# A hybrid encoder block: five convolution pairs by Strassen instead of three, and thirty Lo blocks made during attention

## The chip, the core and the metric

The kernel runs on one core of one Trainium2 chip. A core has TensorE (PE in the profile; its weight loads are PEld), VectorE (DVE), ScalarE (ACT), GpSimd (POOL) and SyncE (SP), each with its own instruction queue, worked off in order, and 16 DMA engines that all queues share. The metric is the device time of one execution in microseconds (us), taken as the median of several runs.

## The reference

One layer over 512 tokens of 2048 numbers, in float32:

```python
u = rms_norm(h, mix_pre_g)
q, k, v, ca, cb, ga, gb = split(u @ w_in)          # 1024, 1024, 1024, 1024, 1024, 2048, 2048 columns
y_attn = neighbourhood_attention(q, k, v, rpb) @ w_attn_o      # 8 heads of 128
z = depthwise_conv31(ca * sigmoid(cb)) + b_dw
y_conv = silu(layer_norm(z)) @ w_conv_o
merged = sigmoid(ga) * y_attn + sigmoid(gb) * y_conv
h = h + rms_norm(merged @ w_out, mix_post_g)
gate, up = split(rms_norm(h, ffn_pre_g) @ w_gate_up)            # 2 x 5632 columns
h = h + rms_norm((silu(gate) * up) @ w_down, ffn_post_g)
```

## The kernel before

Activations lie transposed: 128 features on the partitions, the 512 tokens along the free dimension. A block is 128 output features; its weights are [128, 2048], two halves of 1024 columns (eight 128 x 128 tiles each).

**Hi and Lo.** Every float32 operand is split: Hi is the value rounded by a ScalarE cast to the type fp32r, Lo is what is left, one VectorE subtraction. A plain product needs three matmuls per weight tile: Hi by Lo, Hi by Hi, Lo by Hi (`gemm`, L198 to L202). `wchunk` (L143) loads 1024 columns of weights into one of five `raw` buffers, casts (`whi`, L152) and subtracts (`wlo`, L157), with three buffers for each. After each chunk it calls `taps(rate)`.

**Strassen pairs.** `strassen` (L271) takes two blocks at once. The 2 x 2 halves of the weights (a11, a12 of the first block, a21, a22 of the second) and of the activations are combined in Winograd's form, so that seven products take the place of eight. `merged` puts Hi and Lo of 256 tokens side by side in one tile, so that a product is eight matmuls of 512 columns with Hi of the weights and eight of 256 with Lo. The products of a normal pair in order: 11 (a11), T2 (s2 = s1 - a11), T1 (s1 = a21 + a22, summed by a DMA), T3 (s3 = a11 - a21), 21 (a12), 22 (s4 = a12 - s2), T4 (a22). `halved_weights` (L255) makes Hi and Lo of each of the seven. Between them VectorE adds in PSUM: y += p1 (L329) after T2, z += u2 (L336) after T1, p5 = y + p5 (L342) after T3, and ScalarE copies (L288). With `turn`, T3 and 22 use Lo ahead of Hi. In the first pair of a product (`apart=True`) product 21 comes second, into a bank of its own, and v += p1 (L338) joins it later; there 22 follows T3 directly. Five places have such a first pair: the gates (g), w_out (wo), the FFN's gate and up (f5), and the two parts of w_down (d, twice).

**Stages.** (1) The first four projections of the convolution, while x arrives. (2) Convolution blocks 2 to PLAIN - 1 = 4 as plain pairs cb, ca (loop L534). `conv` (L434) gates a block, `begin_block` (L451) starts its depthwise convolution and queues 30 taps (`todo`); a tap is one VectorE instruction (L473). (3) V in two halves of eight chunks, with `normalize` (L524) making the normalized tiles, four pairs of them (UN_EARLY) ahead of the last plain pair. (4) Eight heads (loop L637): q and k as plain products, then `attention`. The taps of the five blocks run here and before, at `rate` per chunk. (5) Two plain gate blocks, then 17 Strassen pairs (loop L734): convolution blocks 5 to 7, then 14 gate pairs. The convolution inputs of pairs 1 and 2 go to DRAM (`z_d`) and come back when `todo` is short; three or four taps per pair stand behind products that TAP_AT names. (6) 16 attention projections (rate R_Y, then `mean` for the taps that are left, layer norm), 16 convolution projections with the gates and the operands of w_out (`operand_steps`, L849). (7) w_out, (8) the FFN.

**Order.** The program's order is a list schedule: an instruction goes when it is the first in the text that is ready by the scheduler's own model of time. `keep_in_program_order` and `issued_behind` (a plain order of issue, no semaphore) bind it by hand: taps are kept in order, a tap in a pair stands behind a matmul, the loads of the gates behind earlier ones.

Of the kernel before, what the change touches and what calls it, by code (L numbers as in the profile page):

```python
# [25 lines left out]
F32 = mybir.dt.float32  # L26
F32R = mybir.dt.float32r
# [4 lines left out]
P = 128  # L32
# [25 lines left out]
DN_3 = DN_2 + DN_P  # L58

LN_AT = 10  # L60
R_CONV, R_V, R_QK, R_Y = 4, (2, 4), 4, 4
PLAIN = 5
TAP_K, TAP_AT = 2, ((1, 3, 5), (0, 1, 3, 5))
BEFORE = 14
WARM = 17
C0_PARTS = (0, 256), (256, 512), (512, 1024)
# [4 lines left out]
SINGLE, SUMMED = 4, 10  # L71
COPY_AT = 10
RE_EARLY = 11
UN_EARLY, YA_EARLY = 4, 8
SUMMED_AT = 10
C_PRE, C_POST, C_FPRE, C_FPOST, C_LNG, C_LNB, C_BDW, C_WDW = 0, 16, 32, 48, 64, 72, 80, 88
C_N = C_WDW + CT * CW
# [3 lines left out]
def hybrid_block(ctx: ExitStack, tc, xT, vecs, rpb, mask, w_c0, w_qk, w_v, w_gg, w_cg, w_ao, w_co, w_out, w_g0, w_gu, w_dn, w_dl, g_post, out):  # L81
# [32 lines left out]
    def abank(name):  # L114
        return at.tile([P, NT], F32, tag="at", name=name)
# [19 lines left out]
            tc.keep_in_program_order(ins)  # L135

    todo, rate = [], 0

    def wraw(name):
        return wp.tile([P, 1024], F32, tag="raw", name=f"raw_{name}", bufs=5)  # L140

    def wchunk(src, name, parts=((0, 1024),), cast=nc.scalar.copy, raw=None, load=nc.sync.dma_start):
        w = src.shape[-1]  # L143
        loaded = raw is not None
        raw = raw if loaded else wraw(name)[:, :w]
        hi = wp.tile([P, 1024], F32R, tag="whi", name=f"whi_{name}")[:, :w]
        lo = wp.tile([P, 1024], F32R, tag="wlo", name=f"wlo_{name}")[:, :w]
        for s in parts:
            s = slice(*s)
            if not loaded:  # L150
                load(raw[:, s], src[:, s])
            ins = cast(hi[:, s], raw[:, s])  # L152
            if len(parts) > 1:
                tc.keep_in_program_order(ins)
        for s in parts:
            s = slice(*s)
            nc.vector.tensor_tensor(out=lo[:, s], in0=raw[:, s], in1=hi[:, s].bitcast(F32), op=ALU.subtract)  # L157
        taps(rate)
        return hi, lo

    def split(src, name, scale=None, pin=False):
# [21 lines left out]
    def gemm(outs, acts, name, n=None, more=None, cols=slice(0, NT), between=(), pin=False, raw=None, load=nc.sync.dma_start, at=None):  # L183

        n = n or len(acts)
        between = iter(between)
        for c in range(0, n, 8):
            w = min(8, n - c)
            while len(acts) < c + w:
                acts.append(more(len(acts)))  # L190
            for i, (ps, src) in enumerate(outs):
                hi, lo = wchunk(src[:, c * P : (c + w) * P], f"{name}_{i}_{c}", raw=None if c or i else raw, load=load)
                for k in range(w):
                    (at or {}).get((c, i, k), lambda: None)()
# [3 lines left out]
                    mmul = nc.tensor.matmul(ps, hi[:, s], al, start=first, stop=False)  # L198
                    if pin and k == 0:
                        tc.keep_in_program_order(mmul)  # L200
                    nc.tensor.matmul(ps, hi[:, s], ah, start=False, stop=False)  # L201
                    nc.tensor.matmul(ps, lo[:, s], ah, start=False, stop=last)  # L202
                next(between, lambda: None)()

    def interleaved(ps, hi, lo, acts, c, cols=slice(0, NT)):
# [46 lines left out]
        load(raw, w[:, c * 1024 : (c + 1) * 1024])  # L252
        return raw

    def halved_weights(w, name, pin=False, after=None):  # L255

        hi = wp.tile([P, 1024], F32R, tag="whi", name=f"{name}h")
        lo = wp.tile([P, 1024], F32R, tag="wlo", name=f"{name}l")
        ins = nc.scalar.copy(hi, w), nc.vector.tensor_tensor(out=lo, in0=w, in1=hi.bitcast(F32), op=ALU.subtract)  # L259
        for i in ins if pin else ():  # L260
            tc.keep_in_program_order(i)
        if after:
            issued_behind(ins[1], after)
        return hi, lo
# [3 lines left out]
        a11 = quarter(w0, 0, name)  # L268
        return (a11, *halved_weights(a11, name))

    def strassen(w0, w1, op, name, n, s1=None, behind_last=None, first=None, quarters=None, apart=False, turn=True, midway=None, taps_at=(), after=None):  # L271

# [5 lines left out]

        def wsum(a, b, op, i):
            t = stp.tile([P, 1024], F32, tag="S", name=f"{name}s{i}")
            nc.vector.tensor_tensor(out=t, in0=a, in1=b, op=op)
            return t

        def copied(ps, i):
# [49 lines left out]
        nc.vector.tensor_tensor(out=z, in0=z, in1=u2, op=ALU.add)  # L336
# [5 lines left out]
        nc.vector.tensor_tensor(out=p5, in0=y, in1=p5, op=ALU.add)  # L342
        s4 = s2
        nc.vector.tensor_tensor(out=s4, in0=a12, in1=s2, op=ALU.subtract)
# [187 lines left out]

    rate = R_CONV
    for i in range(2, PLAIN):  # L534
        if i == PLAIN - 1:
            for c in range(UN_EARLY):
                normalize(c)
        pb, pa = abank(f"cb{i}"), abank(f"ca{i}")
        gemm([(pb, w_cg[CT + i])], u, f"cb{i}", between=() if i > 2 else (first_convs,))
        gemm([(pa, w_cg[i])], u, f"ca{i}")  # L540
        conv(i, pa, pb)

# [90 lines left out]
        nc.scalar.copy(o, po)  # L633
        nc.gpsimd.dma_start(att_d[h], o)  # L634
# [97 lines left out]

    op = operands(b11, b2, t12, t34)
    for n in range(CT - PLAIN + KT - 2):  # L734
        gate = n >= CT - PLAIN
        i = n - (CT - PLAIN) + 2 if gate else n + PLAIN
        w0, w1 = (2 * CT + i, 2 * CT + KT + i) if gate else (CT + i, i)
        if n:
            s1, quarters = sums(w_cg[w1], f"g{n}", load_in_order) if n == 1 else None, None
        c11, c12, c21, c22 = strassen(  # L740
            w_cg[w0], w_cg[w1], op, f"g{n}", n + 1, s1, quarters=quarters, first=None if n else first, apart=n == 0,
            midway=None if n else plain_gates, taps_at=TAP_AT[n % 2] if n else (),
        )
        if i == KT - 1:

# [775 lines left out]
```

## Time and profile before

| | before |
|---|---|
| three runs, us | 2476.03, 2477.77, 2477.32 (median 2477.32) |
| profiled execution, us | 2478.54 |
| its span, us | 2476.7 |
| mean granted TensorE clock | 0.998 |
| DMA moved, MB | 476.00 |

The span runs from the first to the last instruction of one profiled execution. A line of the profile's groups reads: line, engine, operation, tiles written and read, count, then busy time, the mean of one in ns, and idle time of the engine just before them with what ended it. A line of the waits reads: who, for whom, us in total, times, longest. A line of the order of time reads: start, duration (with matmuls that are alike put together), engine, line, tiles. A stretch's line gives, per engine, busy time and number of instructions, then the clock, the busy share of the DMA engines and GB/s. Where the stages lie, by the starts of TensorE's instructions: first plain pair 51.0, last plain pair 95.6, V 118.6, QK and attention 207.1, plain gates from about 415, first g pair 461.9, y 794.7, first wo pair 972.3, f5 1251, the two d parts 2059 and 2259.

### The profile page before, as it was taken

To read this page: it belongs to the slowest core of one execution; us is meant where nothing else is said; L and a number is where in the kernel's file an instruction comes from. 1 tells how busy PE (TensorE), PEld (TensorE's weight loads), DVE (VectorE), ACT (ScalarE), POOL (GpSimd) and SP (SyncE) were. 2 spreads that over 40 slices of the span, in tenths; PEclk is the share of its full clock that TensorE was granted. 3 is DMA by queue.
4 is the path that set the end of the run, shared out by engine and by line. 5 is a ranking of instruction groups with operands and counts; after the bars stand their busy time and mean duration, and the time that the engine had idled before them with its cause. 6 is when DMAs were issued, how large, how long until landed. Compare 5 with 4: busy or idle time off the path is not lost. (4 is left out here: it accounts for less than half of the span.)

```text
span 2476.7 us, 35648 instructions
## 1 busy us (share of the span) xinstructions
PE 2454.9 (99%) x13219; PEld 2123.7 (86%) x13219; DVE 2080.8 (84%) x2756; ACT 1262.5 (51%) x1951; POOL 481.9 (19%) x574
## 2 busy tenths in 40 slices
PE   9999999999999999999999999999999999999998
PEld 7888888888888887889888888888888888888887
DVE  5998754998989778878998888889988889989886
ACT  5233333655555344556555555555555565556554
POOL 0102312200000000012111111222221203532343
PEclk9999999999999999999999999999999999999999
DMA  6363224866667543769466655667666678888987
GB/s 216 125 205 104 103 90 133 253 189 195 187 196 232 187 140 123 205 211 307 147 178 179 184 174 168 184 199 203 209 210 190 215 226 247 239 224 256 213 222 221
DMA packets 162958, 476.00 MB, mean 192 GB/s; under 512 B 18528, under 2 KB 28224, under 8 KB 162784
## 3 DMA queue, kind: packets, MB, share of 16 engines
q1 hardware_dynamic: 107200, 334.41, 40.4%
q0 software_dynamic: 33840, 101.34, 19.2%
q10 hardware_dynamic: 21744, 37.98, 4.1%
q8 instruction: 104, 1.70, 0.3%
q14 instruction: 70, 0.57, 0.1%
HBM read 400.52 MB, written 72.22 MB: 191 GB/s over the span
## 5 line engine op out<-in xcount | busy, mean ns | idle before, releaser
L473 DVE SCALAR_TENSOR_TENSOR cv<-z,vec,cv 128x497 f32<-128x497 f32 (+9 forms) x180 | 137.7, 766 | 2.8
L1058 POOL TENSOR_TENSOR row<-row,asq 128x512 f32<-128x512 f32 x30 | 55.0, 1832 | 406.6 <-ACT asq L1057 406.6
L157 DVE TENSOR_TENSOR wlo_qk<-raw_qk,whi_qk 128x1024 fp32r<-128x1024 f32 x32 | 39.9, 1247 | 57.3 <-ACT whi_qk L152 57.3
L1219 POOL TENSOR_TENSOR ys<-ys,row 128x512 f32<-128x512 f32 x32 | 57.7, 1802 | 119.6 <-DVE ys L355 109.2
L152 ACT CAST whi_qk<-raw_qk 128x1024 fp32r<-128x1024 f32 x32 | 33.6, 1051 | 81.2 <-PE qk L201 44.4
L1082 POOL TENSOR_TENSOR an<-an,row 128x512 f32<-128x512 f32 x32 | 54.0, 1688 | 72.8 <-DMA an<-a_d 46.4
L152 ACT CAST whi_y<-raw_y 128x1024 fp32r<-128x1024 f32 x31 | 32.6, 1052 | 66.4 <-PE py L201 50.9
L572 POOL TENSOR_TENSOR bm<-braw,msk 128x64 f32<-128x64 f32 x96 | 47.1, 526 | 17.3 <-DMA braw<-in_rpb 17.3
L198 PE MATMUL py<-ycl,whi_y 128*128 128x512 f32 x128 | 49.8, 389 | 0.0
L201 PE MATMUL py<-ych,whi_y 128*128 128x512 f32 x128 | 49.8, 389 | 0.0
L202 PE MATMUL py<-ych,wlo_y 128*128 128x512 f32 x128 | 49.8, 389 | 0.0
L157 DVE TENSOR_TENSOR wlo_y<-raw_y,whi_y 128x1024 fp32r<-128x1024 f32 x31 | 37.8, 1221 | 10.6 <-ACT whi_y L152 10.3
L473 DVE SCALAR_TENSOR_TENSOR cv<-zr,vec,cv 128x497 f32<-128x497 f32 (+14 forms) x60 | 45.2, 755 | 0.5
L483 POOL TENSOR_TENSOR csum<-csum,cv 128x512 f32<-128x512 f32 x7 | 12.6, 1803 | 158.9 <-DVE cv L473 149.1
L823 DVE TENSOR_TENSOR gg<-py,gg 128x512 f32<-128x512 f32 x32 | 21.7, 684 | 18.4 <-PE py L202 10.6
L609 ACT ACTIVATE sc<-sc,st 128x256 f32<-128x256 f32 x32 | 16.1, 505 | 31.0 <-DVE st L608 30.2
L1220 POOL DMA_DIRECT2D y_d<-ys x32 | 29.0, 907 | 10.1 <-POOL ys L1219 7.8
L1149 DVE TENSOR_TENSOR sg<-sg,su 128x512 f32<-128x512 f32 x39 | 30.0, 768 | 0.0
L634 POOL DMA_DIRECT2D att_d<-ao x8 | 4.4, 554 | 127.2 <-ACT ao L633 107.0
L201 PEld LDWEIGHTS py<-ych,whi_y 128*128 128x128 f32 x128 | 24.0, 188 | 5.0
L202 PEld LDWEIGHTS py<-ych,wlo_y 128*128 128x128 f32 x128 | 24.0, 188 | 5.0
L198 PEld LDWEIGHTS py<-ycl,whi_y 128*128 128x128 f32 x128 | 24.0, 188 | 4.9
(3251 smaller groups left out, 8656.5 us busy)
## 6 DMA issues: line engine op xcount, KB each, us to landing
raw_qk<-in_w_qk SPq DMA_DIRECT2D x32, 512.0 KB, 3.4
a_d<-sg ACTq DMA_DIRECT2D x41, 256.0 KB, 4.0
raw_v<-in_w_v SPq DMA_DIRECT2D x16, 512.0 KB, 5.2
gg<-g_d SPq DMA_DIRECT2D x32, 256.0 KB, 4.9
raw_y<-in_w_co SPq DMA_DIRECT2D x16, 512.0 KB, 3.6
raw_f<-in_w_g SPq DMA_DIRECT2D x16, 512.0 KB, 4.2
an<-a_d POOLq DMA_DIRECT2D x32, 256.0 KB, 5.5
as_d<-an POOLq DMA_DIRECT2D x32, 256.0 KB, 4.8
```

Of the source, the lines that this page charges most:

```text
L152: ins = cast(hi[:, s], raw[:, s])
L157: nc.vector.tensor_tensor(out=lo[:, s], in0=raw[:, s], in1=hi[:, s].bitcast(F32), op=ALU.subtract)
L198: mmul = nc.tensor.matmul(ps, hi[:, s], al, start=first, stop=False)
L201: nc.tensor.matmul(ps, hi[:, s], ah, start=False, stop=False)
L202: nc.tensor.matmul(ps, lo[:, s], ah, start=False, stop=last)
L473: ins = nc.vector.scalar_tensor_tensor(out=a[:, to], in0=z[:, fr], scalar=col(C_WDW, i * CW + w), in1=a[:, to], op0=ALU.mult, op1=ALU.add)
L572: nc.gpsimd.tensor_tensor(out=bm[:, o + i - i0], in0=raw[:, :, min(max(i, 0), 3) * EC : (min(max(i, 0), 3) + 1) * EC], in1=msk[:, o + i - ...
L1058: nc.gpsimd.tensor_tensor(out=row[n], in0=row[n], in1=sq, op=ALU.add)
L1082: ins = nc.gpsimd.dma_start(t, a_d[DN_P + k]), nc.gpsimd.tensor_tensor(out=t, in0=t, in1=row[k // KT], op=ALU.mult)
L1149: nc.vector.tensor_tensor(out=t, in0=t, in1=up, op=ALU.mult)
L1219: tc.keep_in_program_order(nc.gpsimd.tensor_tensor(out=t, in0=t, in1=row[n], op=ALU.mult))
L1220: tc.keep_in_program_order(nc.gpsimd.dma_start(y_d[0, o], t, accum_op=ALU.add))
```

## The change

- PLAIN goes from 5 to 3: convolution blocks 3 and 4 leave the plain loop and become Strassen pairs, of which there are now 19 (5 convolution, 14 gate).
- With three plain blocks, 90 instead of 150 taps belong to the stages up to attention. R_V goes from (2, 4) to (1, 4). When no taps are left there, `wchunk` calls `lo_ahead` instead: it takes up the blocks loaded at the call before (a ScalarE copy to fp32r, a VectorE subtraction, a store by GpSimd to `lo_d`) and loads the next one or two of them (alternating), each behind the last matmul of the chunk before. 30 blocks: a12 and a22 of pairs 1 to 18, without the first three and the last three.
- In the pairs, those blocks' Lo is loaded from `lo_d` by SP instead of being subtracted by VectorE.
- The 150 taps of the five convolution pairs: TAP_AT names six or seven products per pair (four in pairs 1 and 18); 112 taps run there, 32 in the y stage, 6 in `mean`.
- UN_EARLY goes from 4 to 2, and the early tiles are normalized between cb and ca of the last plain pair.
- VectorE's order in the five first pairs: the Lo of s3 and v += p1 behind y += p1; s4 behind z += u2; the following pair's s2 and s3 behind z += u2.
- Four of the operand steps of w_out for the last tile but one are put ahead of the last gate.

```diff
-R_CONV, R_V, R_QK, R_Y = 4, (2, 4), 4, 4
-PLAIN = 5
-TAP_K, TAP_AT = 2, ((1, 3, 5), (0, 1, 3, 5))
+R_CONV, R_V, R_QK, R_Y = 4, (1, 4), 4, 4
+AHEAD_PER_CHUNK = 1, 2
+PLAIN = 3
+TAP_K, TAP_AT = 2, ((0, 1, 2, 3, 4, 5), (0, 1, 2, 3, 4, 5, 6), (0, 2, 3, 5))
...
-UN_EARLY, YA_EARLY = 4, 8
+UN_EARLY, YA_EARLY = 2, 8
...
+    lo_d = dr.tile([CT - PLAIN + KT - 2, 2, P, 1024], F32, name="lo_d")
+    ahead_of_pairs, loaded, latest, with_pairs = [], [], [None], False
+
+    def lo_ahead():
+
+        for dst, t in loaded:
+            h = sm.tile([P, 1024], F32R, tag="jh", name="jh", bufs=1)
+            for ins in (
+                nc.scalar.copy(h, t),
+                nc.vector.tensor_tensor(out=t.bitcast(F32R), in0=t, in1=h.bitcast(F32), op=ALU.subtract),
+            ):
+                issued_behind(ins, latest[0])
+            nc.gpsimd.dma_start(dst, t)
+        count = AHEAD_PER_CHUNK[len(ahead_of_pairs) % 3 == 0]
+        loaded[:] = []
+        for dst, src in ahead_of_pairs[:count]:
+            t = sm.tile([P, 1024], F32, tag="jr", name="jr", bufs=3)
+            issued_behind(nc.sync.dma_start(t, src), latest[0])
+            loaded.append((dst, t))
+        del ahead_of_pairs[:count]
...
-        taps(rate)
+        if todo or ahead or waiting:
+            taps(rate)
+        elif with_pairs:
+            lo_ahead()
...
-    def halved_weights(w, name, pin=False, after=None):
+    def halved_weights(w, name, pin=False, after=None, lo_src=None):
...
+        if lo_src is not None:
+            nc.scalar.copy(hi, w)
+            nc.sync.dma_start(lo.bitcast(F32), lo_src)
+            return hi, lo
...
         def wsum(a, b, op, i):
             t = stp.tile([P, 1024], F32, tag="S", name=f"{name}s{i}")
-            nc.vector.tensor_tensor(out=t, in0=a, in1=b, op=op)
+            ins = nc.vector.tensor_tensor(out=t, in0=a, in1=b, op=op)
+            if held and not apart:
+                issued_behind(ins, held.pop(0))
             return t
...
-        nc.vector.tensor_tensor(out=y, in0=y, in1=p1, op=ALU.add)
+        first_sum = nc.vector.tensor_tensor(out=y, in0=y, in1=p1, op=ALU.add)
         u2 = copied(y, 2)
         s3 = wsum(a11, a21, ALU.subtract, 3)
-        product(y, s3, "T3", lo_first=turn)
+        product(y, halved_weights(s3, name, after=first_sum if apart else None), "T3", lo_first=turn)
...
-        nc.vector.tensor_tensor(out=z, in0=z, in1=u2, op=ALU.add)
+        second_sum = nc.vector.tensor_tensor(out=z, in0=z, in1=u2, op=ALU.add)
         if apart:
-            nc.vector.tensor_tensor(out=v, in0=v, in1=p1, op=ALU.add)
+            held[:] = second_sum, second_sum
+            issued_behind(nc.vector.tensor_tensor(out=v, in0=v, in1=p1, op=ALU.add), first_sum)
             x = v
         else:
-            product(x, a12, "21", last=True)
+            product(x, halved_weights(a12, name, lo_src=lo[0]), "21", last=True)
...
-        nc.vector.tensor_tensor(out=s4, in0=a12, in1=s2, op=ALU.subtract)
+        ins = nc.vector.tensor_tensor(out=s4, in0=a12, in1=s2, op=ALU.subtract)
+        if apart:
+            issued_behind(ins, second_sum)
...
-        product(y, a22, "T4", last=True)
+        product(y, halved_weights(a22, name, lo_src=lo[1]), "T4", last=True)
...
     for i in range(2, PLAIN):
+        pb, pa = abank(f"cb{i}"), abank(f"ca{i}")
+        gemm([(pb, w_cg[CT + i])], u, f"cb{i}", between=() if i > 2 else (first_convs,))
         if i == PLAIN - 1:
             for c in range(UN_EARLY):
                 normalize(c)
-        pb, pa = abank(f"cb{i}"), abank(f"ca{i}")
-        gemm([(pb, w_cg[CT + i])], u, f"cb{i}", between=() if i > 2 else (first_convs,))
...
-    rate = R_QK
+    for n in range(1, CT - PLAIN + KT - 2):
+        ahead_of_pairs += [(lo_d[n, j], w_cg[w][:, 1024:]) for j, w in enumerate(pair_of(n)[2:])]
+    del ahead_of_pairs[:3]
+    del ahead_of_pairs[-3:]
+    rate, with_pairs = R_QK, True
...
-            midway=None if n else plain_gates, taps_at=TAP_AT[n % 2] if n else (),
+            midway=None if n else plain_gates, taps_at=TAP_AT[2 if n in (1, 18) else n % 2] if n else (),
+            lo=[lo_d[n, j] if 3 <= 2 * (n - 1) + j < 33 else None for j in range(2)],
...
-        mr[i] = gated(*projected(i, 1, w_co, yc))
+        now = projected(i, 1, w_co, yc)
+        if i == KT - 1:
+            for _ in range(4):
+                next(steps[HT - 2])
+        mr[i] = gated(*now)
...
-        if i < KT - 2:
-            for _ in range(1 if i < HT else 5):
+        if i < KT - 1:
+            for _ in range(1 if i < HT or i == KT - 2 else 5):
                 next(steps[i % HT])
     for _ in range(5):
-        for c in (HT - 2, HT - 1):
-            next(steps[c])
+        next(steps[HT - 1])
```

More of the change, by code (lines that the diff above doesn't have):

```diff
@@ L201, in gemm @@
                     nc.tensor.matmul(ps, hi[:, s], ah, start=False, stop=False)
-                    nc.tensor.matmul(ps, lo[:, s], ah, start=False, stop=last)
+                    latest[0] = nc.tensor.matmul(ps, lo[:, s], ah, start=False, stop=last)
                 next(between, lambda: None)()
@@ L269, in begun, with strassen @@
         return (a11, *halved_weights(a11, name))
-    def strassen(w0, w1, op, name, n, s1=None, behind_last=None, first=None, quarters=None, apart=False, turn=True, midway=None, taps_at=(), after=None):
+    held = []
+    def strassen(w0, w1, op, name, n, s1=None, behind_last=None, first=None, quarters=None, apart=False, turn=True, midway=None, taps_at=(), after=None, lo=(None, None)):
         x, y, z = ((bank, abank)[n % 2](f"{name}_{i}") for i in range(3))
@@ L634, in attention, with pair_of @@
         nc.gpsimd.dma_start(att_d[h], o)
-    rate = R_QK
+    def pair_of(n):
+        gate = n >= CT - PLAIN
+        i = n - (CT - PLAIN) + 2 if gate else n + PLAIN
+        return gate, i, *((2 * CT + i, 2 * CT + KT + i) if gate else (CT + i, i))
+    for n in range(1, CT - PLAIN + KT - 2):
[3 more added lines that the diff above has]
+    rate, with_pairs = R_QK, True
     for h in range(H):
@@ L644, in hybrid_block @@
         attention(h, *qk, bm)
-    assert not todo
-    rate = 0
+    assert not todo and not ahead_of_pairs and not loaded
+    rate, with_pairs = 0, False
     sm_ctx.close()
@@ L734, in hybrid_block @@
     for n in range(CT - PLAIN + KT - 2):
-        gate = n >= CT - PLAIN
-        i = n - (CT - PLAIN) + 2 if gate else n + PLAIN
-        w0, w1 = (2 * CT + i, 2 * CT + KT + i) if gate else (CT + i, i)
+        gate, i, w0, w1 = pair_of(n)
         if n:
```

## The prediction

> **What bounds the kernel now.** I read the page first, then PE's waits, then TensorE's order of time, then the busy time by stretch, and last the DMA list.
>
> ```profile
> span 2476.7 us, 35648 instructions
> PE 2454.9 (99%) x13219; PEld 2123.7 (86%) x13219; DVE 2080.8 (84%) x2756; ACT 1262.5 (51%) x1951; POOL 481.9 (19%) x574
> ...
> PE po L629 <- DVE ptl L627: 1.5, 2, 0.8
> PE wo L302 <- DVE wo0v L342: 1.4, 1, 1.4
> PE d L302 <- ACT d_0v L288: 1.3, 1, 1.3
> PE pv L560 <- DVE un15l L166: 1.2, 1, 1.2
> PE wo L302 <- DVE m L180: 0.9, 1, 0.9
> PE wo L302 <- ACT wo0v L288: 0.6, 1, 0.6
> ...
> PE ca L202 <- DVE wlo_ca L157: 0.5, 1, 0.5
> ...
> PE g L302 <- DVE g L336: 0.3, 1, 0.3
> PE g L302 <- ACT g0v L288: 0.3, 1, 0.3
> ...
> PE ca L198 <- ACT whi_ca L152: 0.2, 1, 0.2
> ```
>
> TensorE is busy 99% of the span. So there are two ways to gain: fewer TensorE columns, and fewer of these short waits. The waits fall in three places that the change touches: the last plain convolution pair and the V stage (0.5 + 0.2 + 1.2 = 1.9 us), the first Strassen pair of each matrix product (g 0.6, wo 2.9, d 1.3 = 4.8 us), and attention (po, 1.5 us). The view undercounts: it starts a gap at a matmul's modelled end.
>
> ```profile
> 39.72 0.39 PE L215 MATMUL c<-u12l,whi_c 128*128 128x512 f32 x1
> ...
> 49.92 0.39 PE L215 MATMUL c<-u15l,whi_c 128*128 128x512 f32 x1
> ...
> 521.51 2.00 PE L302 MATMUL g<-b,g3h 128*128 128x512 f32 x8
> ...
> 541.02 2.00 PE L302 MATMUL g<-b,g4h 128*128 128x512 f32 x8
> ...
> 986.96 2.00 PE L302 MATMUL wo<-mt,wo0h 128*128 128x512 f32 x8
> 990.33 1.63 PE L302 MATMUL wo<-mt,wo0h 128*128 128x512 f32 x6 [1.37 <-DVE wo0v L342]
> ```
>
> Between the first two rows lie 45 starts: (49.92 - 39.72) / 45 = 0.2267 us for a 512-column matmul. A Strassen pair lasts 541.02 - 521.51 = 19.51 us. In wo the eighth matmul's successor was due at 986.96 + 8 x 0.2267 = 988.77 and began at 990.33: 1.56 us lost where the view says 1.37. So I add 0.2 to each wait: 2.5 us in the V stage (three waits), 6.0 us in the first pairs (six waits).
>
> **1. Two convolution pairs from plain to Strassen.** A plain pair is 2 blocks x 16 x 3 = 96 matmuls of 512 columns: 96 x 0.2267 = 21.76 us. Two of them go (43.52) and two Strassen pairs come (39.02): **-4.5 us**. TensorE has nothing that could hide this, so it is the firmest term.
>
> **2. The early stage.** VectorE makes it wait.
>
> ```profile
> 51.00:72.80 21.80, 21.80 (x101) 18.16 (x102) 13.19 (x18) 7.10 (x9) 7.40 (x4) 1.00 0.17 57
> 72.80:94.90 22.10, 22.10 (x100) 18.28 (x99) 21.61 (x28) 3.69 (x4) 2.15 (x1) 1.00 0.32 111
> 94.90:118.50 23.60, 22.91 (x100) 18.35 (x99) 22.03 (x31) 6.97 (x9) 1.79 (x2) 1.00 0.49 157
> 118.50:163.60 45.10, 43.93 (x195) 36.02 (x194) 42.44 (x58) 17.98 (x25) 4.80 (x3) 1.00 0.78 255
> ...
> L473 DVE SCALAR_TENSOR_TENSOR cv<-z,vec,cv 128x497 f32<-128x497 f32 (+9 forms) x180 | 137.7, 766 | 2.8
> ...
> L157 DVE TENSOR_TENSOR wlo_qk<-raw_qk,whi_qk 128x1024 fp32r<-128x1024 f32 x32 | 39.9, 1247 | 57.3 <-ACT whi_qk L152 57.3
> ...
> L152 ACT CAST whi_qk<-raw_qk 128x1024 fp32r<-128x1024 f32 x32 | 33.6, 1051 | 81.2 <-PE qk L201 44.4 <-issue 23.6 <-PE pv L560 8.8
> ```
>
> After the span and the length, a row's pairs are PE, PEld, DVE, ACT and POOL; the last three numbers are the clock, the DMA share and GB/s. From the first pair to the end of V's first half VectorE works 99.3 of 112.6 us. The change takes out 40 of the 60 taps that belong there (40 x 0.766 = 30.6), eight Lo of the two pairs (8 x 1.25 = 10.0) and two block beginnings of some 2 us: about 55 us stay, in 112.6 - 43.5 - 2.5 = 66.6 us of TensorE. That is 83% instead of 88%, and one tap per V chunk instead of two outweighs two more normalized tiles in the chunks. I expect 2.0 of the 2.5 us back, not all: normalizing now begins some 45 us earlier, right behind the first two convolution blocks, and its x loads pass the second half of the weights on SP's queue and its u_d stores join ACT's. From both sides: -2.5 to +2 (V's first chunk late by two Lo). **-2.0 us.**
>
> **3. Lo made ahead in attention.** 38 taps are left at QK, so ten chunks of 32 still carry taps; twenty calls load 30 blocks (2, 1, 2, 1, ...), a call later ScalarE rounds and VectorE subtracts, and POOL stores.
>
> ```profile
> 335.80:362.00 26.20, 26.20 (x131) 21.59 (x130) 12.03 (x26) 9.07 (x20) 5.27 (x17) 1.00 0.28 96
> ...
> 1097.00:1130.00 33.00, 33.00 (x235) 31.13 (x235) 22.59 (x32) 18.10 (x30) 12.59 (x23) 1.00 0.93 352
> ...
> raw_qk<-in_w_qk SPq DMA_DIRECT2D x32, 512.0 KB, 3.4
> ...
> d_8q<-in_w_dn SPq DMA_DIRECT2D x8, 512.0 KB, 7.4
> ...
> L634 POOL DMA_DIRECT2D att_d<-ao x8: 539/559/559, 245.3 to 428.1; - x8
> ...
> DMA to landing us min/median/max: 2.3/2.3/4.6
> ```
>
> A head lasts 26.2 us, four chunks of 6.55. Six blocks per head add 7.5 us to VectorE (12.0 to 19.5) and 6.3 to ScalarE (9.1 to 15.4): both fit. The bytes: 60 x 0.524 = 31.5 MB over 20 x 6.55 = 131 us, beside 96 GB/s x 131 = 12.6 MB: 337 GB/s, where 352 at a share of 0.93 is the most the trace shows without a TensorE wait. So it fits with little room. Three waits are new: SP waits for one of three jr buffers (behind it: the next weights, five buffers deep), POOL for the subtraction (behind it: the bias adds), ScalarE for the landing (behind it: the weight casts, the split of q and k, Exp). The ring decides: one chunk until the block is taken up (6.55), two casts and one Lo (3.35), the issue (0.56), the landing of the store (2.3 to 4.6): 12.8 to 15.1 us, against the 13.1 us that three buffers for three blocks per two chunks allow. The casts run about two chunks of matmuls ahead (2 x 24 x 0.2267 = 10.9 us), so I let this cost only blocked attention steps: two or three more po-like waits of 0.5. **+1.2 us**; below, -1.0 if fewer taps spare the po waits; above, the third rival.
>
> [...]
>
> **4. Normal pairs and the y stage.**
>
> ```profile
> 580.05:599.56 19.51, 19.51 (x114) 17.21 (x113) 16.99 (x21) 10.79 (x16) 0.88 (x1) 1.00 0.63 189
> ...
> 775.18:794.70 19.52, 19.52 (x115) 17.22 (x114) 19.05 (x27) 14.75 (x23) 0.87 (x1) 1.00 0.80 243
> ...
> L804 DVE TENSOR_TENSOR ycl<-cv,ych x1: 684/684/684, 877.6 to 877.6; 128x512 fp32r<-128x512 f32 x1
> ```
>
> Per pair: three more taps (2.3) and two fewer Lo (2.5): VectorE stays at 17.0. Transfers: 2 x 0.524 MB / 19.51 us = 54 GB/s more, 189 to 243, which is what the last pair carries today with no wait. A loaded Lo waits on SP for one of three wlo buffers, with the next pair's quarters queued behind; it has some 7.4 us (T1, T3 and the Hi half of its product) to land. The last pair gets a fourth tap: 19.05 + 0.77 is over 19.52, and I count **+0.3 us** (0 to +3, if tap and y += p1 collide in many pairs). Six taps instead of two are left for the mean: 3 us later, hidden, since the last ycl stands 7 us before its first use near 885. If that cover is gone it costs up to 3.
>
> **5. VectorE's order in the five first pairs.** It puts y += p1 and z += u2 ahead of work that isn't due, and moves four operand steps of wo ahead of the last gate. That removes the six waits (-6.0). But s4 = a12 - s2 must now follow z += u2. f5's pair, which loses nothing today, prices that:
>
> ```profile
> 1256.34 1.22 DVE L344 TENSOR_TENSOR f5s<-f5q,f5s 128x1024 f32<-128x1024 f32 x1
> ...
> 1262.95 0.70 DVE L336 TENSOR_TENSOR f<-f,f5v 128x512 f32<-128x512 f32 x1 [0.16 <-ACT f5v L288]
> ...
> 1262.34 0.58 ACT L288 COPY f5v<-f 128x512 f32<-128x512 f32 x1
> ...
> 1263.06 2.00 PE L302 MATMUL f<-t,f5h 128*128 128x512 f32 x8
> 1264.90 1.11 PE L302 MATMUL f<-b,f5l 128*128 128x256 f32 x8
> ```
>
> Today s4 (L344) is done at 1257.6, long before product 22 begins at 1264.90. Behind z += u2 it runs 1263.6 to 1264.8, its cast (1.05) ends near 1265.9 and its Lo (1.22) near 1267.1: product 22, Lo first, is 2.2 us late. T4 can go first, as it did in wo's row at 990.33; it waits for p5 = y + p5, which can end 0.2 + 0.70 after T3: 0.95 us late, or up to 1.6 as in wo, when a 1.2 us operation stands ahead. I take 1.2 in each of five pairs, +6.0: together **0.0 us**, between -1.2 (5 x 0.95) and +5.0 (5 x 2.2).
>
> **Sum:** -4.5 - 2.0 + 1.2 + 0.3 + 0.0 = -5.0. The profiled execution took 2478.54 us (span 2476.7); the median of the runs, 2477.32, is 1.2 lower, and the change is carried over to it: **2472.3 us**. Its own range is -8 to -2. About 0.2%, 5 us, is what a measurement of this kernel can tell from no change, so the forecast lies on that edge.
>
> **Rivals.**
> - *The first pairs heal.* If T4 or the next pair's product fills the place of 22, all 6.0 us go: -11.0, 2466.3. For it: each wait of the first pairs names an operation that the edits move forward. Against it: nothing on TensorE is ready between the end of T3 and p5's add. Chance 0.20.
> - *Product 22 keeps its written place.* The s4 chain costs 5 x 2.2 = 11.0 against 6.0 saved: the sum is 0.0, 2477.3. For it: f5's row at 1264.90 is 22, ahead of T4. Against: wo's row at 990.33 is T4, ahead of 22, when s4 was late. Chance 0.20.
> - *Slower: the ring of three jr buffers.* With loads landing as d_8q's (7.4 instead of within the 6.55 chunk) and stores at 4.6, a turn takes 15.1 + 0.85 = 16.0 instead of 13.1 us: 2.9 us in each of ten pairs of chunks, 29 us, less the 10.9 us that casts run ahead: +18, in place of the 1.2: +11.9, 2489.2. It decides from a turn of 14.2 us on, and makes the kernel slower by over 0.2% from about 15.3. For it: 337 of 352 GB/s. Against it: landings of 3.4 and 2.3 us in this stage today. [...] Chance 0.13.
> - *The loaded Lo arrive late in the pairs,* so that the stored blocks gain nothing: 1 us in 16 pairs, +16: -5.0 + 16 = +11.0, 2488.3. For it: d_8q's 7.4 us is as long as the time a load has. Against: the last g pair's 243 GB/s without a wait. Chance 0.05.
>
> **How the numbers follow.** Forecast 0.42. Faster by over 0.2%: 0.24 of the forecast, all of the first rival, 0.03 of the second: 0.47. Slower: 0.09 of the third, 0.04 of the fourth, 0.03 of the second: 0.16. The rest, 0.37, is within 0.2%. The range 2465.8 to 2482.0 takes in the first two rivals and the near part of the others; some 0.05 lies below, 0.12 above.
>
> **What would show it.** Right: cb and ca last one pair, the first g pair starts about 45 us earlier, no wait on un15l, normal g pairs still 19.5 us apart, DMA near 330 GB/s in the last five heads; in every first pair one gap of 1 to 1.6 us ahead of T4 or 22, f5's too. Wrong: f5's pair without a gap (then s4 isn't the price), ACT casts of jh that wait for a landing with TensorE idle behind them, or gaps in the normal pairs that name a lo_d load.

## The result and the profile after

The changed kernel took 2534.94 us (median, 2534.61 to 2539.04) where before took 2477.55 in the same session: ratio 1.0236, interval 1.0221 to 1.0252. It is 57 us slower; the prediction had said 2472.3, and no case in it reached beyond 2489.2. The profiled execution took 2535.16 us with a span of 2533.1.

The page's first block and TensorE's waits (engine, line, what it waited for: us in total, times, longest) after the change:

```profile
span 2533.1 us, 36056 instructions
PE 2467.4 (97%) x13251; PEld 2132.3 (84%) x13251; DVE 2103.8 (83%) x2780; ACT 1300.7 (51%) x1999; POOL 499.7 (20%) x606
```

```profile
PE s L629 <- DVE qk_1l L190: 33.4, 4, 8.9
PE pv L593 <- ACT un4h L190: 4.7, 1, 4.7
PE d L334 <- ACT d_0h L287: 2.7, 2, 1.8
PE g L334 <- DVE g1s L313: 1.9, 1, 1.9
PE f L334 <- ACT f5h L287: 1.8, 1, 1.8
PE pmu L821 <- POOL csum L518: 1.7, 1, 1.7
```

Before, no wait was above 1.5 us. Now four waits in attention hold 33.4 us, and the waits that the change was to remove (un15l's 1.2, g's two of 0.3, d_0v's 1.3) have gone and others stand in their place. Where the 56.4 us of span lie is best read from the starts of TensorE's stages in the traces. Each number is us from the first matmul of one stage to that of the next; the four right columns belong to experiments told below.

| stage | before | after | no Lo ahead | order alone | order without s4 | last version |
|---|---|---|---|---|---|---|
| third plain pair (cb) to projections | 156.1 | 117.5 | 118.4 | 155.9 | 156.1 | 109.9 |
| attention (first qk to plain gates) | 206.8 | 245.7 | 205.0 | 206.8 | 206.8 | 205.1 |
| first g pair | 20.6 | 23.2 | 21.7 | 23.2 | 19.6 | 20.7 |
| other g pairs (16; with three plain pairs 18) | 312.2 | 354.8 | 355.4 | 312.2 | 312.5 | 351.7 |
| y up to its second half | 90.6 | 93.9 | 93.9 | 90.6 | 90.6 | 91.1 |
| first wo pair | 23.7 | 23.5 | 22.9 | 24.8 | 24.0 | 22.1 |
| f5's pair | 19.5 | 21.6 | 21.6 | 21.6 | 19.6 | 19.5 |
| first pair of each d half | 40.6 | 43.8 | 43.8 | 43.8 | 39.2 | 40.3 |

Attention alone lost 38.9 us. One of its four waits, on POOL (start, us, what ran, and in brackets the idle time before it with its releaser):

```profile
258.17 0.54 POOL L669 DMA_DIRECT2D att_d<-ao  x1 [2.83 <-ACT ao L668]
263.16 6.32 POOL L607 TENSOR_TENSOR bm<-braw,msk 128x64 f32<-128x64 f32 x12 [4.45 <-DMA braw<-in_rpb]
269.43 1.62 POOL L151 DMA_DIRECT2D lo_d<-jr  x3
```

and on ScalarE:

```profile
277.52 1.04 ACT L147 CAST jh<-jr 128x1024 fp32r<-128x1024 f32 x1 [11.03 <-DMA jr<-in_w_cg]
278.47 0.58 ACT L190 CAST qk_1h<-qk 128x512 fp32r<-128x512 f32 x1
```

This is the chain. POOL stands in the bias adds: 4.45 us waiting for their load and 6.32 us of adding. Three finished Lo wait behind it, to be stored at 269.43. All three jr buffers are held by them, so SP's next load must wait; ScalarE's next instruction is the cast of that load and idles 11.03 us; and behind the cast stands the split of qk_1, without which the scores `s` can't start. SP's waits count how often the ring held a load (times in the middle), and ScalarE's how the wait went on:

```profile
SPq L156 <- DMA lo_d<-jr: 75.1, 21, 9.9
```

```profile
ACT jh L147 <- DMA jr<-in_w_cg: 49.0, 7, 12.4
```

The stretches around that gap (us, busy time of PE, PEld, DVE, ACT, POOL; then the granted clock, DMA share, GB/s):

```profile
271.60:280.30 8.70, 0.41 (x2) 0.00 (x0) 1.71 (x2) 2.48 (x3) 0.18 (x1) 0.68 0.99 360
280.30:284.00 3.70, 3.43 (x14) 3.37 (x15) 3.37 (x9) 0.92 (x4) 0.76 (x5) 0.50 0.79 292
284.00:288.00 4.00, 4.00 (x18) 3.08 (x18) 3.06 (x10) 2.90 (x9) 0.53 (x1) 0.88 0.44 156
250.00:420.00 170.00, 136.57 (x644) 114.71 (x643) 88.54 (x150) 68.39 (x118) 52.52 (x112) 0.89 0.69 240
```

In the gap the DMA engines are full (0.99), which speaks for too many bytes; over the stage they move 240 GB/s at 0.69, which speaks against. After the gap TensorE's granted clock is 0.50 over 3.7 us and 0.88 over the next 4, by which it loses some 2 us more. Four times that, less the 1.5 us of po's waits that were there before, is about what the 38.9 us have beyond the 33.4 of the four waits.

V shows another loss, on VectorE:

```profile
83.44 1.23 DVE L178 TENSOR_TENSOR wlo_v<-raw_v,whi_v 128x1024 fp32r<-128x1024 f32 x1
85.85 0.69 DVE L478 TENSOR_TENSOR z<-ca,sg 128x512 f32<-128x512 f32 x1 [1.17 <-POOL sg L473]
86.45 0.74 DVE L508 SCALAR_TENSOR_TENSOR cv<-z,vec,cv 128x509 f32<-128x509 f32 x1
87.11 0.54 DVE L489 TENSOR_SCALAR cv<-z,vec 128x512 f32<-128x512 f32 x1
87.57 0.75 DVE L508 SCALAR_TENSOR_TENSOR cv<-z,vec,cv 128x510 f32<-128x510 f32 x1
88.23 0.75 DVE L564 SCALAR_TENSOR_TENSOR un<-xn,vec,r 128x512 f32<-128x512 f32 x1
```

The last row makes un4. It stands behind the third block's gate, its beginning and two taps, and TensorE, which needs un4 from 85.2 on, waits 4.7 us for it.

### The profile page after: what moved, and what is told of

Same layout as the page of the kernel before. It is cut to its first block, busy times and chain, and to the rows that moved or that the text cites. A ratio compares the mean times of both kernels' runs of the same rounds, so it can differ in the third digit from the quotient of the medians.

```text
span 2533.1 us, 36056 instructions
## 1 busy us (share of the span) xinstructions
PE 2467.4 (97%) x13251; PEld 2132.3 (84%) x13251; DVE 2103.8 (83%) x2780; ACT 1300.7 (51%) x1999; POOL 499.7 (20%) x606
## 3 DMA queue, kind: packets, MB, share of 16 engines
q0 software_dynamic: 38608, 118.64, 20.7%
## 4 chain that ended last, share of the span: by engine, by line
PE 89%; DVE 3%; DMA 3%; issue 1%; POOL 1%; ACT 1%; SPq 0%; DVEq 0%; ACTq 0%; POOLq 0%
PE f L334 30%; PE g L334 14%; PE d L334 12%; PE wo L334 5%; PE pd L1206 3%; PE f L239 2%; PE qk L225 2%; PE qk L226 2%; PE qk L222 2%; PE c L239 2%; PE py L222 1%; PE py L225 1%; PE py L226 1%; PE pl L1363 1%; PE pv L595 1%
## 5 line engine op out<-in xcount | busy, mean ns | idle before, releaser
L508 DVE SCALAR_TENSOR_TENSOR cv<-z,vec,cv 128x497 f32<-128x497 f32 (+14 forms) x120 | 92.5, 772 | 1.7
L508 DVE SCALAR_TENSOR_TENSOR cv<-zr,vec,cv 128x497 f32<-128x497 f32 (+14 forms) x120 | 91.0, 762 | 0.5
L148 DVE TENSOR_TENSOR jr<-jr,jh 128x1024 fp32r<-128x1024 f32 x30 | 37.5, 1252 | 48.5 <-ACT jh L147 48.5
L147 ACT CAST jh<-jr 128x1024 fp32r<-128x1024 f32 x30 | 31.4, 1047 | 51.7 <-DMA jr<-in_w_cg 49.0
L607 POOL TENSOR_TENSOR bm<-braw,msk 128x64 f32<-128x64 f32 x96 | 49.8, 553 | 15.2 <-DMA braw<-in_rpb 15.1
L629 PE MATMUL s<-qk_1l,qk_0h 128*128 128x256 f32 x32 | 11.9, 373 | 33.4 <-DVE qk_1l L190 33.4
L629 PEld LDWEIGHTS s<-qk_1l,qk_0h 128*128 128x128 f32 x32 | 8.1, 254 | 36.0 <-issue 35.6
L867 DVE TENSOR_TENSOR gg<-py,gg 128x512 f32<-128x512 f32 x32 | 21.7, 686 | 16.0 <-PE py L226 9.6
L151 POOL DMA_DIRECT2D lo_d<-jr x30 | 16.1, 539 | 91.5 <-DVE jr L148 61.3
L334 PE MATMUL d<-d,d_0h 128*128 128x512 f32 x112 | 29.0, 402 | 2.7 <-ACT d_0h L287 2.7
```

The source lines that it names most:

```text
L334: mmul = nc.tensor.matmul(ps[:, cols], wt[:, ws[k]], t[:, cols], start=first and n + k == 0, stop=last and n + k == HT, skip_group_check=True,
L508: ins = nc.vector.scalar_tensor_tensor(out=a[:, to], in0=z[:, fr], scalar=col(C_WDW, i * CW + w), in1=a[:, to], op0=ALU.mult, op1=ALU.add)
```

## The experiments

**Attention.** Theory: the order on POOL and the turn of the ring cause the gaps. Rival: the bytes do, since 337 GB/s were wanted. Two kernels keep every byte. The first gives the ring a fourth buffer and, to make room, takes the second buffer from the bias and its load:

```
-  t = sm.tile([P, 1024], F32, tag="jr", name="jr", bufs=3)
+  t = sm.tile([P, 1024], F32, tag="jr", name="jr", bufs=4)
-  raw = sm.tile([P, ROWS, 4 * EC], F32, tag="braw", name=f"braw{h}", bufs=2)
+  raw = sm.tile([P, ROWS, 4 * EC], F32, tag="braw", name=f"braw{h}", bufs=1)
-  bm = sm.tile([P, 12, ROWS, EC], F32, tag="bm", name=f"bm{h}", bufs=2)
+  bm = sm.tile([P, 12, ROWS, EC], F32, tag="bm", name=f"bm{h}", bufs=1)
```

> The bytes, the queues and the order of every engine stay as in the changed kernel; the ring of jr has four buffers, and bm and braw have one each to make room. Theory (order): the gaps of 8 to 9 us in attention come from the turn of the ring, since POOL's lo_d stores stand behind the bias adds. A fourth buffer gives each load a third of 13.1 us, 4.4 us, more: the four gaps of 34.1 us in all fall to 17 or less, attention from 245.8 to 228 us or less, the run from 2535 to 2518 or less. Rival (bandwidth): the transfers of the Lo made ahead are too many for the DMA engines; the same bytes give the same gaps, attention 244 to 248 us, the run 2532 to 2538.

It took 2512.73 us, ratio 1.0139 (1.0124 to 1.0154): 22 us less than the changed kernel, attention 222.5. Its waits:

```profile
PE po L664 <- DVE ptl L662: 12.1, 4, 3.7
```

The second leaves the ring at three and issues a head's bias adds one head earlier:

```
-  for h in range(H):
-      bm = bias_of(h)
+  bms = [bias_of(0)]
+  for h in range(H):
...
           qk.append(split(ps, f"qk{h}_{i}"))
+          if i == 0 and h + 1 < H:
+              bms.append(bias_of(h + 1))
-      attention(h, *qk, bm)
+      attention(h, *qk, bms[h])
```

> The ring keeps three buffers and the bytes stay; the twelve bias adds of a head are issued on POOL one head earlier, in the middle of the projections, with their load's wait. Theory (order): the stores no longer wait for 4.5 us of a bias load and 6.3 us of adds at the end of a head, so the gaps of 8 to 9 us go or fall under 2 us each: attention 207 to 216 us, the run 2495 to 2508. What could spoil it: the adds now stand ahead of other stores in the middle of the head, and a gap of some 2 to 4 us moves there. Rival (bandwidth): same bytes, same gaps, the run 2532 to 2538.

It took 2506.01 us, ratio 1.011 (1.0095 to 1.0125), attention 218.1. The waits of this stage:

```profile
PE s L629 <- DVE qk_1l L190: 8.2, 4, 3.9
...
PE po L664 <- DVE ptl L662: 2.8, 2, 2.3
```

Either edit takes away more than half of the gaps with the same transfers, which run at 272 and 276 GB/s over 250 to 400 us there, where the changed kernel has 246. So for this larger part the bytes are not the cause. The second is a little short of what I expected (207 to 216): the adds now stand ahead of other stores. Against the 205.0 us that attention takes without these transfers (next experiment), 17.5 and 13.1 us remain. How much of that is order and how much is transfers is open: in the gap shown above, the load that came last took 5.0 us to land (272.45 to 277.44), where loads of its size took 3.4 before. Whether both edits together would close the gaps wasn't tried.

**What the Lo made ahead is worth.**

```
-  del ahead_of_pairs[:3]
-  del ahead_of_pairs[-3:]
+  ahead_of_pairs.clear()
...
-  lo=[lo_d[n, j] if 3 <= 2 * (n - 1) + j < 33 else None for j in range(2)],
```

> No Lo is made in attention; the pairs subtract their Lo on VectorE as before, with the changed kernel's six or seven taps. Both theories expect attention at 205 to 208 us as before, 39 us less. What the run tells is what the Lo made ahead is worth in the pairs: VectorE has 17.0 us of work in a normal pair of 19.5 us, and two subtractions of 1.25 us more make 19.5. If VectorE then keeps up, the pairs stay at 19.5 to 19.8 us and the run is 2496 to 2501; if it doesn't, each of the 15 pairs loses about 1 us and the run is near 2511.

2494.4 us, ratio 1.0065 (1.0049 to 1.0082), a little under the 2496 to 2501 expected. Attention is back at 205.0, and the g pairs, which now subtract all their Lo themselves, take 355.4 us instead of 354.8. Thirty blocks made ahead had saved 0.6 us. VectorE had the time:

```profile
600.00:619.50 19.50, 19.50 (x114) 17.21 (x113) 18.82 (x25) 10.78 (x15) 0.86 (x1) 1.00 0.63 196
```

It works 18.82 of 19.50 us in a pair, and TensorE works all of them. So the largest part of the change removed work that cost nothing.

**The first pairs.** The whole order of VectorE put into the kernel before, and then the same without one edit. Both also have the change's four operand steps of w_out ahead of the last gate.

```
   ins = nc.vector.tensor_tensor(out=s4, in0=a12, in1=s2, op=ALU.subtract)
-  if apart:
-      issued_behind(ins, second_sum)
```

> The kernel before, with nothing of the change but VectorE's order in the five first pairs. Theory: the order is what made the first pairs 7.8 us longer in the changed kernel, since s4, put behind z += u2, brings product 22 and T4 late by about 2 us a pair; here too they grow by 6 to 8 us, and the run is 2484 to 2487 where before is 2478. The prediction's sum was 0.0 for this part: 2478 within 1. Rival: part of the 7.8 us came from the changed convolution's work beside it in g; then this run is 2 to 3 us below the theory's.

> As the run with the order alone, without the one edit that puts s4 behind z += u2. If s4's place is the whole price, the six waits of the first pairs go and nothing comes for them: 6 us faster than before, 2472. If other edits of the order cost too (T3's Lo behind y += p1, the next pair's sums behind z += u2), it lies between, 2474 to 2480.

The order alone: 2489.23 us against 2478.37, ratio 1.0045 (1.0032 to 1.0058), so 10.9 us slower, which is more than either case. Without s4's place: 2479.16, ratio 1.0002 (0.9993 to 1.0011). So s4 behind z += u2 costs 10.1 us, 2.0 a pair in the mean; by the table it is between 0.8 (wo) and 3.6 us (g). The rest of the order brings nothing: it removes waits and makes others, as the second kernel's rows show:

```profile
PE wo L306 <- DVE m L180: 1.5, 1, 1.5
PE wo L306 <- DVE wo0l L259: 1.3, 1, 1.3
...
PE wo L306 <- DVE mt L180: 1.0, 1, 1.0
PE d L306 <- ACT d_2v L292: 0.9, 2, 0.5
```

g's 0.6 us is gone and d's 1.3 became 0.9, but wo's 2.9 became 3.8. What g's and d's first pairs gain by it (1.0 and 1.4 us) is lost again in the pairs right behind the first ones of g, f and d, which take 19.80, 19.85, 20.28 and 20.25 us instead of 19.5 (2.1 us in all). How s4 costs 2.0 us is seen in f5's pair of the changed kernel, on VectorE,

```profile
1312.03 0.70 DVE L368 TENSOR_TENSOR f<-f,f5v 128x512 f32<-128x512 f32 x1
1312.64 1.21 DVE L377 TENSOR_TENSOR f5s<-f5q,f5s 128x1024 f32<-128x1024 f32 x1
1313.77 1.22 DVE L313 TENSOR_TENSOR f6s<-f6s,f6q 128x1024 f32<-128x1024 f32 x1
1314.90 0.69 DVE L375 TENSOR_TENSOR f5v<-f,f5v 128x512 f32<-128x512 f32 x1
```

on ScalarE,

```profile
1313.94 1.04 ACT L287 CAST f5h<-f5s 128x1024 fp32r<-128x1024 f32 x1 [1.94 <-DVE f5s L377]
1314.89 1.04 ACT L287 CAST f5h<-f5q 128x1024 fp32r<-128x1024 f32 x1
```

and on TensorE.

```profile
1312.15 2.00 PE L334 MATMUL f<-t,f5h 128*128 128x512 f32 x8
1315.99 1.45 PE L334 MATMUL f<-t,f5h 128*128 128x512 f32 x5 [1.83 <-ACT f5h L287]
```

T4 does go first, at 1315.99. But its weights, a22, are cast second, behind s4's cast, which idles 1.94 us for s4. The late s4 holds T4's cast too, so nothing is left that could fill the gap; and p5's add (1314.90) is late as well, since the next pair's sum (f6s) is put right behind s4.

**V.** First, more tiles made early and fewer taps before V:

```
-R_CONV, R_V, R_QK, R_Y = 4, (1, 4), 4, 4
-UN_EARLY, YA_EARLY = 2, 8
+R_CONV, R_V, R_QK, R_Y = 2, (1, 4), 5, 4
+UN_EARLY, YA_EARLY = 3, 8
```

> Three x pairs are normalized ahead of V instead of two, and two taps instead of four stand in each chunk before V (five instead of four in attention's chunks take up the rest). Theory: the gap of 4.9 us at 85 us comes from VectorE's order, in which the ninth... fifth normalized tile stands behind sg, z and three taps; it goes, the projections start at 112.5 to 114 us instead of 117.5, and the run falls by 4 to 5 us, to 2530 or 2531. Rival: VectorE is full from 51 us on, so the gap only moves into the last convolution pair, and the run stays within 1.5 us of 2535.

2535.65 us, ratio 1.0233 (1.0218 to 1.0248): no gain in the run. From V's first matmul to the projections it is 91.7 instead of 94.7 us, but the wait has only moved, to un6 (2.3 us); attention, with its fifth tap, took 247.7 instead of 245.7, and f5's pair 23.2 instead of 21.6 (of which the last section).

**A version that keeps what works.** Two kernels drop the Lo made ahead, the order of the first pairs and the moved operand steps, move taps from the early stage into attention, and take five taps a chunk in y. One has three plain pairs, the other four:

```
-R_CONV, R_V, R_QK, R_Y = 4, (1, 4), 4, 4
-UN_EARLY, YA_EARLY = 2, 8
+R_CONV, R_V, R_QK, R_Y = 1, (0, 2), 3, 5
+UN_EARLY, YA_EARLY = 4, 8
...
-PLAIN = 3
-TAP_K, TAP_AT = 2, ((0, 1, 2, 3, 4, 5), (0, 1, 2, 3, 4, 5, 6), (0, 2, 3, 5))
+PLAIN = 4
+TAP_K, TAP_AT = 2, ((0, 1, 2, 3, 5), (0, 1, 2, 3, 5), (0, 1, 3, 5))
```

(PLAIN and TAP_AT are changed only in the one with four; there R_CONV, R_V and R_QK are 3, (1, 3) and 4.)

> The changed kernel with three plain pairs, without Lo made ahead, with before's order in the first pairs, with 19 taps instead of 52 ahead of attention (three a chunk in attention) and four x pairs normalized early, and with five taps instead of four a chunk in y. If each loss belongs to the edit that I name for it: the V stage falls from 95 to 89 to 91 us, the first pairs from 7 over to level with before, y from 93.9 to 90.6 to 91.4; only the 3 to 4 us of crowded taps in the normal pairs stay against the 4.5 us of two convolution pairs: 2476 to 2480 where before is 2478. Rival: fewer taps don't mend V, since its x loads or the gate of the third block set the gap: 5 us more.

> As the run with three plain pairs, but with four: one convolution pair by Strassen more than before, five taps a normal pair, 36 taps for y. The gain is half, 2.25 us; if VectorE then keeps up in the normal pairs (18.2 of 19.5 us by the sum of its operations), nothing is lost there: 2475 to 2477 where before is 2478. If the crowded taps cost in its pairs too, 2477 to 2480.

2472.94 us, ratio 0.9981 (0.9972 to 0.9990), and 2473.65, ratio 0.9981 (0.9971 to 0.9990). Both are faster than I expected (2476 to 2480, and 2475 to 2477). With three plain pairs V takes 88.7 us, with four 87.0, and y 90.6 in both, about as expected. In both the normal pairs lose: with four plain pairs, the last 15 take 296.0 instead of 15 x 19.51 = 292.7. A tap in T1 is what VectorE does right ahead of y += p1, as in this pair of the changed kernel:

```profile
728.62 0.75 DVE L508 SCALAR_TENSOR_TENSOR cv<-zr,vec,cv 128x509 f32<-128x509 f32 x1
729.28 0.69 DVE L361 TENSOR_TENSOR g<-g,g13v 128x512 f32<-128x512 f32 x1
```

and TensorE's order there has three matmuls of product 21 between T1's Lo (729.70) and T3's Lo (731.48):

```profile
729.70 1.11 PE L334 MATMUL g<-t,g13l 128*128 128x256 f32 x8
730.65 0.86 PE L334 MATMUL g<-b,g13h 128*128 128x512 f32 x3
731.48 1.22 PE L334 MATMUL g<-t,g13l 128*128 128x256 f32 x8
732.54 0.63 PE L334 MATMUL g<-t,g13h 128*128 128x512 f32 x2
```

The three take 0.83 us from start to start, where 3 x 0.2267 is 0.68, and the eight behind them 1.06, where the eight of T1 take 0.95: 0.26 us more together, about what this pair lasts beyond 19.51. The add had ended at 729.97, and the profile has no wait here. So it is the order of the instructions that costs, and not a wait for the add; why a change of product in the middle is dear isn't shown. In the changed kernel 12 of the 18 pairs have a tap right ahead of y += p1, and these 12 last 19.76 to 19.82 us.

So the next two kernels have no tap in T1 (number 2):

```
four plain pairs:
-TAP_K, TAP_AT = 2, ((0, 1, 2, 3, 5), (0, 1, 2, 3, 5), (0, 1, 3, 5))
+TAP_K, TAP_AT = 2, ((0, 1, 3, 4, 5), (0, 1, 3, 4, 5), (0, 1, 3, 5))
three plain pairs:
-R_CONV, R_V, R_QK, R_Y = 1, (0, 2), 3, 5
+R_CONV, R_V, R_QK, R_Y = 1, (0, 2), 3, 6
-TAP_K, TAP_AT = 2, ((0, 1, 2, 3, 4, 5), (0, 1, 2, 3, 4, 5, 6), (0, 2, 3, 5))
+TAP_K, TAP_AT = 2, ((0, 1, 3, 4, 5, 6), (0, 1, 3, 4, 5, 6), (0, 1, 3, 5))
```

> As the run with four plain pairs; in every normal pair the tap that stood in T1 stands in product 21 instead, so that y += p1 is not behind it. Theory: T3's Lo half, which comes first, waits 0.24 us in each of 15 pairs for y += p1 alone; the pairs fall from 19.76 to 19.51 us, and the run by 3.4 us to 2470.2. Rival: VectorE is full, and the tap in 21 makes p5's add or 22 late instead: 2473 to 2475.

> As the run with three plain pairs; no tap in T1, six taps in every normal pair, and six taps a chunk in y for the 44 that are left. Theory: the pairs lose their 0.22 us, 3.5 us in all: 2469.5. Rivals: VectorE is full with six taps and seven Lo (19.5 of 19.5 us), and gaps elsewhere in the pairs take the place: 2472 to 2476; or six taps a chunk make y late, as six taps left for the mean did: 2 to 3 us more.

Four: 2470.88 us, ratio 0.9973 (0.9962 to 0.9984); its 15 pairs take 294.2, so half of the loss went. The other half is in three pairs: two of 19.8 and 19.9 us, and the last with 20.35, where TensorE now waits 0.6 us for a copy on ScalarE. Three: 2474.76, ratio 0.9987 (0.9978 to 0.9996): the 16 pairs came down from 315.7 to 312.7, as expected, but six taps a chunk made y 94.0 us long, and 3.4 went out again there. The last two keep five taps a chunk in y and put two more taps in the second and the last pair; one of them goes back to two x pairs made early:

```
-R_CONV, R_V, R_QK, R_Y = 1, (0, 2), 3, 6
+R_CONV, R_V, R_QK, R_Y = 1, (0, 2), 3, 5
-TAP_K, TAP_AT = 2, ((0, 1, 3, 4, 5, 6), (0, 1, 3, 4, 5, 6), (0, 1, 3, 5))
+TAP_K, TAP_AT = 2, ((0, 1, 3, 4, 5, 6),) * 3
-UN_EARLY, YA_EARLY = 4, 8      (the second kernel alone)
+UN_EARLY, YA_EARLY = 2, 8
```

> As the run with three plain pairs and no tap in T1, but with six taps in the second and the last pair too, so that 42 are left for y, and five a chunk there: two stay for the mean, as before the change. Theory: the pairs keep the 3 us that the move gained and y comes back from 94.0 to 90.6 us: 2470 where before is 2478. Rival: the last pair, where the first ya tiles are split beside it, has no room for two taps more: 1 to 2 us lost there, 2471 to 2472.

> As the run beside it, but with two x pairs normalized ahead of V, as in the changed kernel. It tells the two mends of V apart. If the taps ahead of V were what made the normalized tiles late, the V stage stays at 88.5 to 89.5 us; if it is the number of tiles made early, a gap of 4 to 5 us at the third x pair comes back and V takes 93 to 95 us.

2471.28 us, ratio 0.9971 (0.9961 to 0.9982), and 2468.95, ratio 0.9962 (0.9948 to 0.9976). The first lies where its rival put it, but not by the rival's cause: the last pair takes 19.5 us, and it is the second that is 0.8 longer. The second kernel is the fastest of all, 8.9 us under before. By the table its gain beyond the two pairs' 4.5 lies mostly in the early stage (2.8 us), attention (1.7) and the first wo pair (1.6); why the last two gained wasn't traced. V there takes 87.0 us without any wait, so the taps ahead of V and in its first half were the cause and not the number of tiles made early; four x pairs made early, as in the other kernel, even cost 1.6 us (88.6, with a wait of 1.1 on un8). The stretch of V's start, in the changed kernel,

```profile
74.30:96.00 21.70, 16.98 (x67) 13.19 (x66) 19.26 (x28) 6.50 (x9) 2.19 (x1) 0.92 0.65 212
```

and in the last version:

```profile
74.40:96.00 21.60, 21.60 (x97) 17.86 (x97) 15.57 (x21) 9.51 (x13) 1.29 (x1) 1.00 0.85 287
```

VectorE has 15.57 us of work instead of 19.26, and TensorE doesn't stop.

## Why the prediction was wrong

- **Two pairs by Strassen, -4.5.** Right, as far as it can be told from the other terms: no run has it alone. In the last version the early stage is 46.3 us shorter and two more g pairs cost 39.5 (351.7 - 312.2), where 43.5 and 39.0 were reckoned. Half of that version's 8.9 us is this term.
- **Early stage, -2.0.** Wrong: the stage from cb on is 38.6 us shorter where 43.5 were to go, a loss of 4.9. The wait on un15l went, as said. I had compared VectorE's busy share over the whole stage (83% after 88%). The stage's beginning was the tight place: there the normalized tiles come due one chunk apart, and taps, gate and block beginning stand between them in one order. My upper bound, V's first chunk late by two Lo, was too small and in the wrong chunk. With 33 taps fewer put ahead of attention in the program (19 instead of 52; by the traces 25 instead of 59 run before its first matmul) the stage is 46.3 us shorter (156.1 - 109.9): the forecast of some 2 us beyond the 43.5 is then met.
- **Lo made ahead, +1.2.** This is the step that failed, by 38 us. Its mechanism was my third rival's, at a chance of 0.13, and even that rival had +18 us where attention lost 38.9. Two things in the step were wrong. First, I named the bias adds as what is queued *behind* POOL's store and never as what stands *ahead* of it. The ring's turn of 12.8 to 15.1 us had the store's issue (0.56) and its landing, but not the 4.45 + 6.32 us for which POOL was in the adds. Second, I let the casts that run two chunks ahead cover a late block, 10.9 us. They may cover the weights. They do not cover the split of q and k, which I had named as queued behind ScalarE's wait and then not priced: it is due at once, and TensorE stood still four times for 7.7 to 9.0 us. The rival's bytes were not the cause of the larger part of the gaps. The step also had no term for the lower clock behind each gap (0.50 to 0.54), some 2 us. The sign that I had named for this, casts of jh that wait for a landing with TensorE idle behind, is what came.
- **What a store costs POOL.** The upper end of my range, 2482.0, allowed for stores that make the ring's turn 2.5 us longer, which no run shows. The 30 stores, in a stage where VectorE worked 88.5 of 170 us, took 531 to 571 ns each, 539 in the mean, where the att_d stores before took 539 to 559; the store was late, not long:

```profile
L151 POOL DMA_DIRECT2D lo_d<-jr x30 | 16.1, 539 | 91.5 <-DVE jr L148 61.3
```

- **Normal pairs, +0.3 (up to +3).** The collision of the tap with y += p1 is there in 12 of 18 pairs, and it cost more than the upper bound: 354.8 - 18 x 19.51 = 3.6 us. It costs by the order of TensorE's instructions, though, and not by a wait for the add. Two Lo fewer per pair brought 0.6 us.
- **y, 0 (up to 3).** The cover was gone, and it cost a little over the bound, 3.3 us. The length of y goes with its last tap, which begins 46.1 us after y's first matmul before and 49.2 us after the change (50.1 in the kernel with six taps a chunk, where y takes 94.0); TensorE waits 1.7 us for POOL's csum behind it.
- **First pairs, 0.0 (-1.2 to +5.0).** Wrong on both sides. +6.0 for s4 should have been +10.1: I let T4 go first at 0.95 to 1.6 us, and did not follow a22's cast, which stands behind s4's on ScalarE. And the -6.0 for six waits was nothing in the run's time: of 4.8 us in the view, 4.7 came back in other rows. I counted each wait that an edit aims at as gone and looked for what is late next in s4's case only.

The mistakes have one form. I priced each new wait by the two instructions that it joins. What cost the time was the queue in which they stand: adds ahead of a store, a split behind a cast, a cast behind a cast, a tile behind taps.

## What to carry to other kernels

Before a ring of buffers is trusted, walk each engine's order through one whole turn and add everything that stands *ahead* of the instruction that frees the buffer, its own waits included; a queue that is idle 80% of the time (POOL here) can still be shut for 11 us just then. Work that an engine with room already hides is worth nothing when it is moved (0.6 us for 30 subtractions of 1.25), however busy the engine looks. And an edit that puts an operation later is priced at the last consumer behind it on the next engine too.

## What the runs showed of the hardware

Behind pauses of TensorE of some 2 us the granted clock over the next 4 us was 0.57 to 0.66 in some cases and 1.00 in others. In f5's pair the changed kernel and the one with the adds moved run the same instructions and pause alike: 1.83 us in TensorE's order of time in the first, as shown above (1315.99), and in the second

```profile
1287.76 2.03 PE L334 MATMUL f<-t,f5h 128*128 128x512 f32 x5 [1.83 <-ACT f5h L287]
```

The 4 us behind the pause, with the clock third from the end, in the changed kernel

```profile
1316.00:1320.00 4.00, 4.00 (x21) 3.46 (x22) 4.00 (x5) 0.89 (x1) 0.00 (x0) 1.00 0.44 161
```

and in the one with the adds moved:

```profile
1287.80:1291.80 4.00, 4.00 (x15) 3.52 (x16) 4.00 (x5) 0.86 (x1) 0.00 (x0) 0.57 0.45 157
```

One kept its clock (1.00) and the pair took 21.6 us; the other had 0.57 over these 4 us and took 23.2, 1.5 us more. The same stands behind g's first pair, 23.2 us with the clock at 0.60 behind its pause and 21.7 without Lo made ahead, where it stayed at 1.00. In the kernel with the order alone, the 4 us behind the pauses of g's first pair, of f5's pair and of the first pair of d's second half read:

```profile
478.00:482.00 4.00, 4.00 (x15) 3.54 (x16) 4.00 (x5) 0.86 (x1) 0.00 (x0) 0.57 0.88 170
1270.80:1274.80 4.00, 4.00 (x22) 3.44 (x23) 4.00 (x5) 0.81 (x1) 0.00 (x0) 1.00 0.45 155
2283.00:2287.00 4.00, 4.00 (x16) 3.53 (x17) 4.00 (x5) 0.87 (x1) 0.05 (x1) 0.64 0.94 198
```

There s4's place costs 3.6 us in g and 3.5 in that pair of d, where the clock fell, and 2.0 in f5, where it didn't: so some 1.5 us of the larger prices can be clock. The four pauses of 7.7 to 9.0 us in the changed kernel's attention were all followed by some 4 us at 0.50 to 0.54.

The traces together have 28 pauses of 2.1 to 2.7 us from one start of TensorE to the next. Behind 14 of them the clock over the next 4 us is 0.57 to 0.66, behind the other 14 it is 1.00. Behind all 17 longer ones (3.2 to 9.3 us) it is 0.50 to 0.62. Nine of these 45 are the changed kernel's: four of 2.10 to 2.25 us, with 0.61 and 0.66 behind two and 1.00 behind the other two, and five of 5.11 to 9.26 us, with 0.50 to 0.57 behind them.

Why like pauses differ no run here shows. Pauses of some 2 us were enough for the lower clock in half of the cases, so these measured rows are what to plan with.
